# A two-layer attention and retention trunk on one core: norm weights moved from the tokens to the weights' rows, shorter rotary tables, a reordered first supertile

## The chip, the cores and the metric

The kernel runs on one core of a Trainium2 chip. Time is device microseconds of one execution. Before the change three runs took 2111.25 to 2114.31 us, median 2113.38. A change of 0.2% or less cannot be told from none.

The engines are called here as the profile calls them: PE (TensorE) multiplies matrices, DVE (VectorE) and ACT (ScalarE) work elementwise, POOL (GpSimd) too, and SP (SyncE) issues nearly all DMAs from its queue. Each engine works through its own instructions in order and waits for others by semaphores.

## The reference, cut to what matters

```python
D_MODEL = 1024; SEQ = 2048; DEPTH = 2; CHUNK = 64        # one batch
# per layer: 8 attention heads of 64, 4 retention heads of 128, w_in (1024, 4096), w_out (1024, 1024)

def rms_norm(x, gain=None):
    y = x * lax.rsqrt(jnp.mean(x * x, axis=-1, keepdims=True) + EPS)
    return y if gain is None else y * gain

def hybrid_layer(x, norm_gain, w_in, w_out, rel_bias, cos, sin):
    hn = rms_norm(x, norm_gain)
    aq, ak, av, ag, rq, rk, rv, rg = jnp.split(hn @ w_in, 8, axis=-1)
    ya = chunked_rel_attention(aq, ak, av, rel_bias)     # own chunk and 8 to the left, softmax
    yr = chunkwise_retention(rq, rk, rv, cos, sin)       # rotary on q and k, decaying state, RMS norm
    y = concatenate([ya * silu(ag), yr * silu(rg)], axis=-1)
    return x + y @ w_out

def reference(x, positions, norm_gain, w_in, w_out, rel_bias, final_gain):
    cos, sin = rotary_tables(positions, 128)             # angle = position * inverse frequency
    for layer in range(DEPTH):
        x = hybrid_layer(x, norm_gain[layer], w_in[layer], w_out[layer], rel_bias[layer], cos, sin)
    return rms_norm(x, final_gain)
```

The norm's weights multiply the columns of hn, which are the rows of w_in in the product: (n * gain) @ w is n @ (gain[:, None] * w).

## The kernel before

**Tiling.** There are 16 token tiles of 128 rows and four supertiles of 512 tokens (index n). The heads are cut into four groups s, each with two attention heads and one retention head. The main loop runs over layer l, group s and supertile n. Every large product is made in two float16 halves for accuracy: a matrix is split into an upper half (wh, hTh) and the rest (wl, hTl), and each product has three terms, upper by upper, upper by lower, lower by upper, over eight blocks of 128 rows (kt): 24 matmuls of 512 columns.

**Stages of one (l, s, n).** dense_T (line 608) makes q and k of attention and of retention with the weights as the stationary operand (matmuls of line 730; the first supertile of all goes by single token tiles, line 712, for its first two sections). evacuate copies each result out; for the retention sections it also turns q and k by the rotary tables: swap (line 664) loads the two halves exchanged by DMA, turn multiplies and adds on POOL (lines 670 to 672), upper, lower and third split the result, tokens transposes k. dense_V (line 737) makes the values and gates (matmuls of line 750). attention (line 776) and retention (line 863) of the supertile before run interleaved with these products: a unit of attention every three rounds, a round being eight dense matmuls.

Attention's unit: scores on PE (lines 798, 799), bias and maximum on DVE (802), exp and upper half on ACT (805, 807), lower half on POOL (808), a transposing DMA (810), and two units later the product with v on PE (818 to 820). A retention step multiplies k and q (line 853), masks the product on DVE (872), takes its upper half on ACT (857) and the rest on DVE (861), and multiplies these by v on PE (853 again).

**Order by hand.** PE, ACT, DVE and POOL run in program order. later(k, fn) puts an instruction k rounds ahead, and push(gen, steps) queues background work, of which run pulls a share in each round. SP's order is left to the scheduler, which issues a DMA as soon as its buffer is free, except up to the first supertile's dense_V, where it is program order as well.

**Background work.** prep_T and prep_V load the next group's eight weight sections of 128 columns (512 KB each; three buffers, w4), square them for a scale (309), sum the squares over partitions with a small matmul (323), and split them in two halves (330 on ACT, 333 on DVE). prep_T of the next group starts at n = 1, prep_V at n = 3; prep_V_next and a half-loading prep_T do it for the next layer during the output product. prep_Omax sums the squares of w_out from eight loads, pushed at s = 2, n = 0, and prep_O splits it. bias_scratch and bias_tiles make the group's bias tiles: a DMA spreads the bias in DRAM (564), another loads a skewed tile (577), POOL sets two corners (579, 580), ACT scales it (581); they are due in n = 0 of each group.

**Norms.** x is loaded by token tile, squared on ACT, and the root taken by POOL (212). Then DVE multiplies the tile by the root and by the gain row, which lies on all partitions as gains[l].b (line 254 for tokens 0 to 7, 1168 for 8 to 15, 986 for layer 1), and the product is split in halves and transposed: tokens 0 to 3 on PE, the others of layer 0 by two DMAs (236, 237); layer 1 by either. gain_scale (line 161) makes a power-of-two scale from the gain, which enters the root (g.m, g.e) and every section's inverse scale (g.i).

**Tables.** tables(n) computes sine and cosine of a supertile's angles in 17 steps on a 128 x 256 tile, mostly on DVE, in three to four floats' precision, stores them to DRAM by eight DMAs, and dense_T loads them back (616, 617).

**The start.** Up to the first dense_V everything is in one list of steps written out by hand (line 1348): x for tokens, W and V for sections, sq, hi, lo and so on for what is done, t for a step of the first tables, d for a step of dense_T, r for the bias's reversal. What follows (line 1353) is a list of 12 rounds beside the first dense_V, with tokens 4 to 7 and steps u of the second tables.

Of the kernel before, what the change touches and what calls it, by code (L numbers as in the profile page):

```python
# [27 lines left out]
def hybrid_trunk(ctx: ExitStack, tc: tile.TileContext, x, pos, gain, gcol, w_in, w_out, rel, fgain,  # L28
# [33 lines left out]
    pool.memset(mhalf, -0.5)  # L62
    invf_sb = cp.tile([P, 1], F32, tag="invf", name="invf_sb")
# [19 lines left out]
    def tables(n, wk):  # L83
# [15 lines left out]
        dve.tensor_copy(ang, pi)  # L99
        dve.tensor_scalar(ang, ang, invf_sb[:, 0:1], None, op0=ALU.mult)  # L100
# [6 lines left out]
        dve.tensor_scalar(k2, k, -(PD + PE_), None, op0=ALU.mult)  # L107
        dve.tensor_tensor(k2, k2, ang, op=ALU.add)
# [7 lines left out]
        dve.tensor_scalar(k, ang, HALF_PI, -TWO_PI, op0=ALU.is_gt, op1=ALU.mult)  # L116
# [19 lines left out]
    TAB_STEPS = 19  # L136
# [5 lines left out]
    def norm_scale(sq, nm, ig=None, k=14):  # L142
# [7 lines left out]
        if ig is not None:  # L150
            dve.tensor_tensor(i.bitcast(F32), i.bitcast(F32), ig, op=ALU.mult)
        return s.bitcast(F32), i.bitcast(F32)

    gains = {}

    def gain_load(l):
        g = gains[l]
        g.b = cp.tile([P, D], F32, tag="gb", name=f"gb{l}")
        sp.dma_start(g.b, gain[l:l + 1, :].to_broadcast([P, D]))

    def gain_scale(l):

        g = gains[l] = St()
        small = lambda tag, w=1, t=F32: b2.tile([P, w], t, tag=tag, name=f"{tag}{l}", bufs=1)
        m, gk = small("gsq", KT), small("gsk", KT)
        ss, i2, e2 = small("gss"), small("gs2", 1, I32), small("gs3", 1, I32)
        raw = gsb[:, l * KT:(l + 1) * KT]
        dve.tensor_tensor_reduce(out=m, in0=raw, in1=raw, scale=1.0, scalar=0.0, op0=ALU.mult, op1=ALU.add, accum_out=ss)
        mb = lowp(ss, f"g{l}")
        yield  # L170
        s_, i_ = norm_scale(allsum(mb, f"g{l}", 2.0 ** -60), f"g{l}", None, -1)
        g.i = b2.tile([P, 1], F32, tag="gi", name=f"gi{l}")
        dve.tensor_copy(g.i, i_)
        dve.tensor_scalar(gk, raw, s_[:, 0:1], None, op0=ALU.mult)
        dve.tensor_tensor(gk, gk, gk, op=ALU.mult)
        dve.tensor_tensor(gk, gk, gk, op=ALU.mult)
        dve.tensor_tensor_reduce(out=m, in0=gk, in1=gk, scale=1.0, scalar=0.0, op0=ALU.mult, op1=ALU.add, accum_out=ss)
        mb = lowp(ss, f"h{l}")
        yield
        m2 = allsum(mb, f"h{l}", 2.0 ** -60)  # L180
        dve.tensor_scalar(e2, m2.bitcast(I32), 23, None, op0=ALU.logical_shift_right)
        dve.tensor_scalar(e2, e2, 9.0, None, op0=ALU.add)
        dve.tensor_scalar(e2, e2, 3, 23, op0=ALU.logical_shift_right, op1=ALU.logical_shift_left)
        dve.tensor_scalar(i2, e2, float(111 << 23), None, op0=ALU.add)
        g.m = b2.tile([P, 1], F32, tag="gm", name=f"gm{l}")
        g.e = b2.tile([P, 1], F32, tag="ge", name=f"ge{l}")
        dve.tensor_tensor(g.i, g.i, i2.bitcast(F32), op=ALU.mult)
        dve.scalar_tensor_tensor(out=g.m, in0=g.i, scalar=2.0 ** -20 / D, in1=g.i, op0=ALU.mult, op1=ALU.mult)
        dve.scalar_tensor_tensor(out=g.e, in0=g.i, scalar=2.0 ** -20 * EPS, in1=g.i, op0=ALU.mult, op1=ALU.mult)
        yield  # L190
# [17 lines left out]
    def rms_of(ss, m, e, nm):  # L208

        dve.tensor_scalar(ss, ss, m, e, op0=ALU.mult, op1=ALU.add)  # L210
# [28 lines left out]
    class Tok:  # L239
# [10 lines left out]
        def rs(self):  # L250
            self.r = rms_of(self.ss, gains[0].m, gains[0].e, self.nm)

        def mul(self):
            dve.scalar_tensor_tensor(out=self.x, in0=self.x, scalar=self.r[:, 0:1], in1=gains[0].b, op0=ALU.mult,
                                     op1=ALU.mult)
# [10 lines left out]
        def hi(self):  # L266
            if self.rows:
                self.rw = (self.rows[:, 0:D], self.rows[:, D:2 * D])
                act.activation(self.rw[0], self.x, AF.Copy)
                return  # L270
# [3 lines left out]
        def lo(self):  # L274
            if self.rows:
                dve.tensor_tensor(self.rw[1], self.x, self.rw[0], op=ALU.subtract)
                return
# [73 lines left out]
    class Sections:  # L351
# [15 lines left out]

        def square(self, j):
# [3 lines left out]
        def scale(self, j):  # L372
            nm = f"{self.nm}{j}"
            self.sv[j], self.iv[j] = norm_scale(allsum(self.sq[j], nm), nm, gains[self.l].i)
# [7 lines left out]
    def prep_T(l, s, g, halves=False, w=None):  # L382
        w = w or Sections(l, s, g, halves)
        w.load(0)
        yield
        for j in range(4):
            if j < 3:
                w.load(j + 1)
            yield
            w.square(j)  # L390
            yield
            yield
            yield
            w.scale(j)
            yield from w.split(j)

# [17 lines left out]
    def prep_V(l, s, g):  # L414
# [16 lines left out]
        def rest(k):  # L431
            for _ in range(k):
                yield

        ld(0)
        ld(1)
# [825 lines left out]
    for t in range(1, 4):  # L1262
        x_in(t)
# [230 lines left out]
```

## Time and profile before

| | us |
|---|---|
| median of three runs | 2113.38 |
| the profiled execution | 2117.65 |
| its span, first to last instruction | 2115.9 |
| PE busy in the span | 2010.4 |
| DVE, ACT, POOL busy | 1253.8, 1139.1, 679.5 |

The profile is of one execution. A row of the timeline gives the start in us from the span's start, the duration in us, engine, line, operation and tiles, and in brackets how long the engine had been idle before it and what ended that. SPq is SP's queue. A row of the waits gives the total in us, the count and the longest. A row of groups ends with busy us, mean ns of one, and idle time before them. Matmuls overlap, so a matmul's spacing, not its duration, is its cost.

### The profile page before, as it was taken

To read this page: it belongs to the slowest core of one execution; us is meant where nothing else is said; L and a number is where in the kernel's file an instruction comes from. 1 tells how busy PE (TensorE), PEld (TensorE's weight loads), DVE (VectorE), ACT (ScalarE), POOL (GpSimd) and SP (SyncE) were. 2 spreads that over 40 slices of the span, in tenths; PEclk is the share of its full clock that TensorE was granted. 3 is DMA by queue.
4 is the path that set the end of the run, shared out by engine and by line. 5 is a ranking of instruction groups with operands and counts; after the bars stand their busy time and mean duration, and the time that the engine had idled before them with its cause. 6 is when DMAs were issued, how large, how long until landed. Compare 5 with 4: busy or idle time off the path is not lost.

```text
span 2115.9 us, 39456 instructions
## 1 busy us (share of the span) xinstructions
PE 2010.4 (95%) x14014; PEld 1052.1 (50%) x14014; DVE 1253.8 (59%) x3839; ACT 1139.1 (54%) x2522; POOL 679.5 (32%) x701
## 2 busy tenths in 40 slices
PE   6778999999999999988999999999999999999998
PEld 4334555555455555544444555555545555554543
DVE  7677566655565655566653556555656566556643
ACT  7455665556655654555444546554665465446432
POOL 1233333433343433321002343434333433433200
PEclk9899999999999999999999999999999999999999
DMA  8767675558665764699875556555685567548874
GB/s 247 165 119 164 137 164 113 115 110 191 148 113 111 159 158 99 132 197 259 206 187 115 121 103 140 123 124 103 149 186 119 101 137 169 123 101 182 217 193 127
DMA packets 645701, 313.63 MB, mean 148 GB/s; under 512 B 459232, under 2 KB 602080, under 8 KB 645504
## 3 DMA queue, kind: packets, MB, share of 16 engines
q1 hardware_dynamic: 645504, 311.12, 66.5%
q8 instruction: 109, 1.79, 0.4%
q14 instruction: 88, 0.72, 0.1%
HBM read 123.26 MB, written 41.98 MB: 78 GB/s over the span
## 4 chain that ended last, share of the span: by engine, by line
PE 47%; DMA 3%; ACT 2%; DVE 2%; issue 1%; POOL 1%; SPq 1%; POOLq 0%; DVEq 0%; ACTq 0%
PE dT L730 14%; PE dV L750 14%; PE dO L1090 12%; DMA pT<-pq 2%; PE r L853 2%; PE S L799 1%; PE S L798 1%; PE o L818 1%; PE o L819 1%; PE o L820 1%; DVE sc L802 1%; ACT sc L805 0%; ACT pq L807 0%; DMA yhy<-rhy 0%; DMA bias<-toep 0%
## 5 line engine op out<-in xcount | busy, mean ns | idle before, releaser
L808 POOL TENSOR_TENSOR pq<-sc,pq 128x640 f16<-128x640 f32 (+4 forms) x256 | 319.9, 1250 | 930.1 <-ACT pq L807 562.5
L805 ACT ACTIVATE sc<-sc,mq,cT 128x640 f32<-128x640 f32 (+4 forms) x256 | 218.5, 853 | 653.8 <-DVE rl L824 330.4
L730 PE MATMUL dT<-hTh,whT 128*128 128x512 f16 x1008 | 386.0, 383 | 11.9 <-DVE rv L766 7.8
L750 PE MATMUL dV<-wlV,hTh 128*128 128x512 f16 x1024 | 389.1, 380 | 6.9 <-DVE wlV L333 6.9
L750 PE MATMUL dV<-whV,hTh 128*128 128x512 f16 x1024 | 389.3, 380 | 6.2 <-DVE gt L768 6.1
L730 PE MATMUL dT<-hTl,whT 128*128 128x512 f16 x1008 | 386.2, 383 | 4.6 <-DMA hTl<-hTl 2.9
L750 PE MATMUL dV<-whV,hTl 128*128 128x512 f16 x1024 | 389.0, 380 | 0.0
L730 PE MATMUL dT<-hTh,wlT 128*128 128x512 f16 x1008 | 385.7, 383 | 0.0
L730 PEld LDWEIGHTS <-whT 128*128 128x128 f16 x2016 | 195.9, 99 | 236.7 <-issue 20.4
L750 PEld LDWEIGHTS <-hTh 128*128 128x128 f16 x2048 | 197.7, 98 | 223.9 <-DVE gt L768 9.1
L802 DVE CUSTOM_DVE_ANT_0 sc<-S,bias 128x640 f32<-128x640 f32 (+4 forms) x256 | 188.8, 737 | 154.7 <-PE S L799 150.8
L1090 PE MATMUL dO<-whO,yhy 128*128 128x512 f16 x512 | 194.8, 381 | 1.9 <-DMA yhy<-rhy 1.9
L1090 PE MATMUL dO<-whO,yly 128*128 128x512 f16 x512 | 194.6, 380 | 0.8 <-DMA yly<-rly 0.8
L1090 PE MATMUL dO<-wlO,yhy 128*128 128x512 f16 x512 | 194.6, 380 | 0.0
L807 ACT ACTIVATE pq<-sc 128x640 f16<-128x640 f32 (+4 forms) x256 | 171.5, 670 | 11.1 <-DMA pT<-pq 3.0
L1090 PEld LDWEIGHTS <-yhy 128*128 128x128 f16 x1024 | 99.9, 98 | 117.2 <-DMA yhy<-rhy 2.6
L750 PEld LDWEIGHTS <-hTl 128*128 128x128 f16 x1024 | 100.3, 98 | 115.8 <-issue 9.9
L730 PEld LDWEIGHTS <-wlT 128*128 128x128 f16 x1008 | 99.3, 98 | 106.4 <-issue 4.3
L818 PE MATMUL o<-v,pT 128*128 128x65 f16 x1120 | 129.8, 193 | 15.6 <-DMA pT<-pq 15.5
L798 PE MATMUL S<-k,q 128*128 128x128 f16 (+3 forms) x592 | 142.3, 267 | 0.7 <-DVE mq L802 0.7
L818 PEld LDWEIGHTS <-pT 128*128 128x128 f16 x1120 | 105.7, 97 | 51.0 <-DMA pT<-pq 21.5
L819 PE MATMUL o<-v,pT 128*128 128x64 f16 x1120 | 130.0, 195 | 0.0
(350 smaller groups left out, 3499.3 us busy)
## 6 DMA issues: line engine op xcount, KB each, us to landing
q<-qq SPq DMA_DIRECT2D x128, 128.0 KB, 2.5
yyy<-y_d SPq DMA_DIRECT2D x32, 512.0 KB, 4.6
stT<-in_w_in_dram SPq DMA_DIRECT2D x27, 512.0 KB, 4.8
stV<-in_w_in_dram SPq DMA_DIRECT2D x26, 512.0 KB, 4.4
k<-kk SPq DMA_DIRECT2D x128, 64.0 KB, 2.1
swp<-rot SPq DMA_DIRECT2D x64, 128.0 KB, 2.6
tabc<-tab SPq DMA_DIRECT2D x32, 256.0 KB, 2.7
tabs<-tab SPq DMA_DIRECT2D x32, 256.0 KB, 3.1
```

The source lines that it names most:

```text
L730: pe.matmul(ps, w_[:, j, kt, :], h_[:, kt, :], start=(m == 0), stop=(m == 23))
L750: pe.matmul(ps, h_[:, kt, a * P:(a + 1) * P], w_[:, kt, :], start=(m == 0), stop=(m == 23))
L798: pe.matmul(o, st.q[:, hx, 0, cs], k_, start=True, stop=False)
L799: pe.matmul(o, st.q[:, hx, 1, cs], k_, start=False, stop=True)
L802: dve.tensor_tensor_reduce(out=v, in0=S[:, 0:w], in1=g.bias[hx][:, 640 - w:640], scale=1.0, scalar=-3.0e38, op0=ALU.add, op1=ALU.max, accu ...
L805: act.activation(v, v, AF.Exp, bias=m[:, 0:1], scale=g.c[:, 0:1])
L807: act.activation(pq[:, 0:w], v, AF.Copy)
L808: pool.tensor_tensor(pq[:, w:2 * w], v, pq[:, 0:w], op=ALU.subtract)
L818: pe.matmul(o[:, 0:65], u.p[:, b, :], v_[:, 0:65], start=(b == 0), stop=False)
L819: pe.matmul(o[:, 0:64], u.p[:, b, :], v_[:, 65:129], start=False, stop=False)
L853: pe.matmul(out_, w_, m_, start=(i == 0), stop=(i + 1 == len(pairs)))
L1090: pe.matmul(ps, h_[:, kt, :], w_[:, kt, :], start=(m == 0), stop=(m == 23))
```

## The change

1. **Gain on the weights.** A new function multiplies a weight section by the norm's weights, one value per row, on DVE, before its squares are taken. It runs once for each of the 64 sections of w_in. The gain row on all partitions, its loads, gain_scale and the gain's scale in every inverse scale are gone. Tokens are no longer multiplied by the gain: where DMAs transpose them, the split takes the root as a scale and the multiplication is gone (12 tiles of layer 0, 10 of layer 1); where PE does, a one-input multiplication by the root stays (4 and 6).
2. **Tables.** Integer to float and the product with the frequency become one step on ACT; two pairs of DVE steps become one each; the cosine is taken as the sine of a quarter turn less the absolute angle; the negation goes to ACT.
3. **Order of terms.** For the first section of dense_T and the first tile of dense_V all eight blocks of one term come first, then the next term, with the half that is ready last at the end. Elsewhere dense_T takes the lower weights second and the lower tokens third.
4. **The first supertile.** The start's DMAs, its list of steps and the 12 rounds are ordered anew: the first weights before the positions, the table steps later, the swap of retention's k in round 9 and not 5 of dense_V, its upper, lower and transposition after it; the loads of tokens 8 to 11 explicitly in the rounds; retention's steps of this supertile in later rounds.
5. **Preparation.** prep_T loads two sections ahead, prep_V three; their lists are shorter by two steps and one.
6. **w_out's squares** are pushed at n = 2 of s = 2 and not n = 0.

```diff
+    def by_gain(st, k0, k1, l):
+
+        g = gsb[:, l * KT + k0:l * KT + k1].unsqueeze(2).to_broadcast([P, k1 - k0, P])
+        dve.tensor_tensor(st, st, g, op=ALU.mult)
...
-        dve.tensor_copy(ang, pi)
-        dve.tensor_scalar(ang, ang, invf_sb[:, 0:1], None, op0=ALU.mult)
+        act.activation(ang, pi, AF.Copy, scale=invf_sb[:, 0:1])
...
-        dve.tensor_scalar(k2, k, -(PD + PE_), None, op0=ALU.mult)
-        dve.tensor_tensor(k2, k2, ang, op=ALU.add)
+        dve.scalar_tensor_tensor(out=k2, in0=k, scalar=-(PD + PE_), in1=ang, op0=ALU.mult, op1=ALU.add)
...
-        dve.tensor_scalar(k, ang, HALF_PI, -TWO_PI, op0=ALU.is_gt, op1=ALU.mult)
-        yield
-        dve.tensor_tensor(k, k, ang, op=ALU.add)
-        dve.tensor_scalar(k, k, HALF_PI, PI_CL, op0=ALU.add, op1=ALU.min)
+        yield
+        dve.scalar_tensor_tensor(out=k, in0=ang, scalar=-1.0, in1=ang, op0=ALU.mult, op1=ALU.max)
...
-        act.activation(k2, k, AF.Sin)
+        act.activation(k2, k, AF.Sin, scale=-1.0, bias=quarter[:, 0:1])
...
-        dve.tensor_scalar(ang, r, -1.0, None, op0=ALU.mult)
+        act.activation(ang, r, AF.Copy, scale=-1.0)
...
     def prep_T(l, s, g, halves=False, w=None):
         w = w or Sections(l, s, g, halves)
-        w.load(0)
+        for j in range(2):
+            w.load(j)
+            yield
+        w.gain(0)
         yield
         for j in range(4):
+            w.square(j)
+            yield
+            yield
             if j < 3:
-                w.load(j + 1)
-            yield
-            w.square(j)
-            yield
-            yield
+                w.gain(j + 1)
             yield
             w.scale(j)
             yield from w.split(j)
+            if j < 2:
+                w.load(j + 2)
...
+    def in_order(apart, terms):
+
+        return [(kt, w) for w in terms for kt in range(KT)] if apart else [(kt, w) for kt in range(KT) for w in terms]
...
-                    d = 4 if j == 2 and first else 3
-                    later(d, turn)
-                    later(d + 2 if first else d + 3, upper)
-                    later(d + 3 if first else d + 4, lower)
...
+                    elif j == 2:
+                        plan = {4: turn, 11: upper, 12: lower, 13: third}
+                    else:
+                        plan = {3: turn, 5: upper, 6: lower, 7: tokens}
...
-                    later(5 if first else 2, swap)
+                    later(9 if first else 2, swap)
...
-                for (w_, h_) in ((g.h, hh), (g.h, hl), (g.l, hh)):
+            for kt, (w_, h_) in in_order(j == 0, ((g.h, hh), (g.l, hh), (g.h, hl))):
...
-                for (w_, h_) in ((g.vh, hh), (g.vl, hh), (g.vh, hl)):
+            for kt, (w_, h_) in in_order(a == 0, ((g.vh, hh), (g.vh, hl), (g.vl, hh))):
...
+        rounds_ret = (5, 10, 10, 14, 14, 18, 18, 23) if (l, s, n) == (0, 0, 0) else [6 * a + b for a in range(4) for b in (0, 5)]
...
         def mul():
-            u.x = xt if on_pe or rows else psS.tile([P, D], F32, tag="S", name=f"xn{nm}")
-            dve.scalar_tensor_tensor(out=u.x, in0=xt, scalar=u.rs[:, 0:1], in1=gains[l].b, op0=ALU.mult, op1=ALU.mult)
+            dve.tensor_scalar(xt, xt, u.rs[:, 0:1], None, op0=ALU.mult)
...
+    sp.dma_start(gsb, gcol)
     W = Sections(0, 0, g00, False)
-    sp.dma_start(gsb, gcol)
-    gains[0] = St()
-    gain_load(0)
+    W.load(0)
     sp.dma_start(invf_sb, invf)
+    x_in(1)
     t0 = tables(0, [gp.tile([P, 256], F32, tag="gt", name=f"wk{i}") for i in range(4)])
...
+    do("xsq0 xrs0 t xmul0 xtr0 Wgm0 xsq1 Wsq0 xrs1 xhi0 xmul1 Wlp0 Wsc0 xlo0 Whi0 xtr1 t xsq2 Wlo0 xrs2 d Wgm1 xhi1 xmul2 "
+       "Wsq1 xlo1 xtr2 Wlp1 xsq3 Wsc1 d xrs3 xhi2 Wgm2 Whi1 xlo2 Wsq2 xmul3 Wlo1 d t Wgm3 xtr3 r Wsq3 d xhi3 Vgm0 Wlp2 Wsc2 "
+       "xlo3 r d Vsq0 Whi2 Vgm1 Whi3 Wlo2 d Vsq1 Vlp0 Wlo3 Vsc0 bs t d Vhi0 t t d d Vhi1 Vgm2 t Vlo0 t Vsq2 d Vgm3 Vlo1 t Vsq3 "
+       "d Vlp2 t d Tu Vsc2 xsq4 t Vhi2 Vhi3 d t d Vlo2 t Vlo3 xsq5 t d Vu t d xsq6 xrs4 t d Vu t xsq7 d t")
     g00.vdone = 4
...
+    push(rounds(["xhi4 xrs5 xrs6", "xlo4 xrs7", "xdma4 xhi5 bt", "xlo5 xhi6", "xdma5 xlo6", "xdma6 xhi7",
+                 "xlo7", "xdma7 x8", "u x8 bt", "u u x8 bt", "u u x8", "u u bt"]), 12)
...
-                if n == 0 and s == 2:
+                if n == 2 and s == 2:
                     push(prep_Omax(l, go), 13)
```

More of the change, by code (lines that the diff above doesn't have):

```diff
@@ L62, in hybrid_trunk @@
     pool.memset(mhalf, -0.5)
+    quarter = cp.tile([P, 1], F32, tag="quarter", name="quarter")
+    pool.memset(quarter, HALF_PI)
     invf_sb = cp.tile([P, 1], F32, tag="invf", name="invf_sb")
@@ L366, in load, with gain @@
             self.sts.append(load_sec(w_in[self.l, :, o:o + P], f"{self.nm}{j}", self.halves))
+        def gain(self, j):
+            for (st, k0, k1) in self.sts[j]:
+                by_gain(st, k0, k1, self.l)
         def square(self, j):
@@ L455, in prep_V @@
         yield
-        yield from rest(2)
-        m = allsum(m2, f"{nm}2")
-        sv, iv[2] = norm_scale(m, f"{nm}2", gains[l].i)
+        yield
+        sv, iv[2] = norm_scale(allsum(m2, f"{nm}2"), f"{nm}2")
         for _ in V_units(l, s, g, iv, nm):
@@ L474, in prep_V_next @@
             sts.append([(st, 0, KT)])
+        for j in range(2):
+            for (st, k0, k1) in sts[j]:
+                by_gain(st, k0, k1, l)
         yield
+        for j in (2, 3):
+            by_gain(sts[j][0][0], 0, KT, l)
         g.vh = b3.tile([P, KT, 512], F16, tag="wh", name=f"wh{nm}")
@@ L727, in dense_T @@
             m = 0
[L728 to L733 removed]
+            for kt, (w_, h_) in in_order(j == 0, ((g.h, hh), (g.l, hh), (g.h, hl))):
+                pe.matmul(ps, w_[:, j, kt, :], h_[:, kt, :], start=(m == 0), stop=(m == 23))
+                m += 1
+                if m in (8, 16) or (m == 24 and first):
+                    yield
             evacuate(j, ps)
```

176 lines of the change are left out of this document (59 added, 117 removed), and 3 rows, old and new, of the table steps.

## The prediction

> **What bounds the kernel now.** I read the page first, then busy time by stretches.
>
> ```profile
> span 2115.9 us, 39456 instructions
> PE 2010.4 (95%) x14014; PEld 1052.1 (50%) x14014; DVE 1253.8 (59%) x3839; ACT 1139.1 (54%) x2522; POOL 679.5 (32%) x701
> ...
> 0.00:100.00 100.00, 72.92 (x491) 42.48 (x492) 69.32 (x181) 59.03 (x116) 18.88 (x35) 0.93 0.79 208
> 100.00:310.00 210.00, 181.34 (x1290) 94.14 (x1288) 140.54 (x417) 121.86 (x266) 78.27 (x76) 0.95 0.70 147
> 310.00:900.00 590.00, 579.28 (x4293) 309.14 (x4290) 347.83 (x1154) 332.42 (x776) 225.10 (x224) 1.00 0.62 132
> ```
>
> The columns of the last three are PE, PEld, DVE, ACT, POOL, granted clock, DMA share, GB/s. PE is the bound: it idles 2115.9 - 2010.4 = 105.5 us. Of that 27.1 us lie in the first 100 us and 28.7 in the next 210, all in the first supertile group (layer 0, s = 0); the following 590 us, three whole groups, idle 10.7. The multiply-adds are the same before and after (two orders of terms, no fewer), so the change can win only idle time and the slow clock behind it, and lose only by new idle time. The waits of PE, largest first, then name who ends them; the first three rows are of 100 to 310 us, the last of the whole run (total, times, longest):
>
> ```profile
> PE r L853 <- DVE dT L861: 11.7, 5, 5.3
> ...
> PE dT L730 <- DMA hTh<-rhn: 3.0, 1, 3.0
> ...
> PE dT L730 <- DMA hTl<-rln: 1.6, 2, 0.9
> ...
> PE dV L750 <- DVE wlV L333: 6.9, 5, 1.6
> ```
>
> **A, the start, to the first dense_V.** Removed: the load of the gain row to all partitions, ahead of the first weights, and gain_scale, whose last instruction sits at 8.51. Added: eight by_gain.
>
> ```profile
> 4.33 0.59 SPq L294 DMA_DIRECT2D stT<-in_w_in_dram  x1
> ...
> 5.30 0.19 ACT L248 ACTIVATION_READ_ACCUMULATOR hTh<-xa 128x1 f32 x1
> ...
> 8.51 0.15 DVE L189 SCALAR_TENSOR_TENSOR ge<-gi 128x1 f32<-128x1 f32 x1
> ...
> 11.40 1.06 ACT L1225 ACTIVATE whT<-stT 128x1024 f16<-128x1024 f32 x1 [5.92 <-DMA stT<-in_w_in_dram]
> ...
> 15.81 1.03 PE L712 MATMUL dT<-hTh,whT 128*128 128x128 f16 x8 [2.59 <-ACT whT L1307]
> ...
> 20.00:40.00 20.00, 18.19 (x226) 15.00 (x225) 18.99 (x46) 18.31 (x33) 0.69 (x1) 1.00 0.90 273
> ```
>
> The first weights set the first dense matmul, at 15.81. Their load moves from SP's place behind the gain row, invf and the positions to the place behind x0, the gain columns and the mask: some 2 us earlier. One by_gain now stands between landing and square. Its price has no row; the nearest is the two-input 1024-element form:
>
> ```profile
> L254 DVE SCALAR_TENSOR_TENSOR xa<-xa,rsn,gb 128x1024 f32<-128x1024 f32 x2 | 2.6, 1282 | 0.1
> ...
> L333 DVE SCALAR_TENSOR_TENSOR wlT<-stT,sT,whT 128x1024 f16<-128x1024 f32 (+1 forms) x32 | 38.0, 1197 | 6.9 <-ACT whT L330 6.8
> ...
> L93 DVE SCALAR_TENSOR_TENSOR wk<-wk,wk 128x256 f32<-128x256 f32 x8 | 3.4, 420 | 0.1
> ...
> 10.94 0.28 DVE L96 TENSOR_SCALAR wk<-wk 128x256 f32<-128x256 f32 x1
> ```
>
> I take 1.28. A one-input multiply by the row's scale (tokens 0 to 3, six of layer 1) has its row only at 256 elements, 0.28; between four times that (1.12) and the same fixed part as the two-input form (about 0.7, from 0.42 at 256 and 1.28 at 1024) I take 0.7. From 20 to 40 us DVE is busy 18.99 of 20, so DVE decides how soon the eight sections are split. Its sum: +8 x 1.28 = +10.2; four token multiplies shorter by 0.58 = -2.3; gain_scale's place on the path -3.2 (its end near 8.7, to the 5.5 at which x0's squares are done); some eight table steps of 0.42 moved behind the last section's scale, about -3.3; five small products with the gain's scale, at the 0.15 of the row at 8.51, -0.8. Net +0.6, as good as even, so the earlier load can come through in part. **A = -1**; ends -2.3 (only the earlier load counts) and +3 (each by_gain also waits for its section to land). The order "all of one term, then the next" gives the V split's lower halves 16 matmuls of slack, so those don't hold dense_V.
>
> **B, tokens 4 to 7 and the second supertile.**
>
> ```profile
> 57.05 1.36 SPq L236 DMA_TRANSPOSE hTh<-hTh  x1
> ...
> 57.41 1.22 DVE L276 TENSOR_TENSOR hTh<-hTh,hTh 128x1024 f16<-128x1024 f32 x1
> ...
> 64.55 0.48 SPq L666 DMA_DIRECT2D swp<-raw  x1
> ...
> 66.09 1.30 SPq L236 DMA_TRANSPOSE hTh<-hTh  x1
> ...
> 74.94 1.24 SPq L237 DMA_TRANSPOSE hTl<-hTl  x1
> ...
> 76.35 0.58 PE L730 MATMUL dT<-hTh,whT 128*128 128x512 f16 x1 [7.78 <-DVE rv L766]
> 79.87 0.59 PE L730 MATMUL dT<-hTl,whT 128*128 128x512 f16 x1 [2.94 <-DMA hTl<-hTl]
> ...
> 80.68 0.63 PE L730 MATMUL dT<-hTh,whT 128*128 128x512 f16 x1
> 81.10 0.63 PE L730 MATMUL dT<-hTl,whT 128*128 128x512 f16 x1
> ...
> 85.75 0.38 PE L730 MATMUL dT<-hTh,whT 128*128 128x512 f16 x1
> 85.97 0.38 PE L730 MATMUL dT<-hTl,whT 128*128 128x512 f16 x1
> ```
>
> The wait is put down to DVE, but DVE was long done; the transposes were not. Token 5's lower half is ready at 57.41 + 1.22 = 58.63, its transposes go out at 66.09: SP's queue stands behind the swap of line 666, which waits for the buffer of the first rotation. The change moves that swap from round 5 to round 9, behind all eight transposes, and drops the four multiplies ahead of them. Then four pairs of 2.8 us follow 57.05: the last would go out near 68 rather than 75. Against it, the tables' eight stores stand last in the hand-written list now, and the table load, which waits for them, is queued on SP ahead of token 4: I put this at +3. Upper halves arrive 4.3 earlier so; and as the lower halves of the tokens are first needed at the 17th matmul, the wait of 2.94 goes. That is -7.2; ACT does two more table steps in these rounds, so **B = -6**; ends -11 (both waits gone) and +1 (table load later than that, nothing won).
>
> **C, the rest of the group, to 310 us.**
>
> ```profile
> 117.84 2.24 DVE L1168 SCALAR_TENSOR_TENSOR hTl<-hTl,rsn,gb 128x1024 f32<-128x1024 f32 x1
> ...
> 118.96 2.24 POOL L671 TENSOR_TENSOR swp<-swp,tabs 128x512 f32<-128x512 f32 x1
> ...
> 121.39 1.30 DVE L116 TENSOR_SCALAR xb<-xb 128x256 f32<-128x256 f32 x1
> ```
>
> The longest wait for dT (5.3) ends right behind these on DVE's queue: a token multiply, stretched beside POOL's rotation, then two table steps. The change removes eight such multiplies here and some 1.8 us of DVE per table (cast, negation and two steps go to ACT or merge), and spreads the first supertile's retention over later rounds. ACT takes two more steps of about 0.4 per table, beside its own 58% load. Of 11.7 I take 7.5 away; of the waits for transposed tokens, 3.0 + 1.6, all but 0.6, since the upper half no longer waits for the multiply and the lower has 16 matmuls more. After a long wait matmuls start 0.43 apart, later 0.22 (80.68 to 81.10, 85.75 to 85.97): two such stretches less, some six matmuls each at 0.21 (an estimate; the one in B lasts longer), would be -2.6; I take -1.5. 7.5 + 4.0 + 1.5: **C = -13**; ends -19 (11.7 + 3.0 + 1.6 + 2.6) and 0.
>
> [...]
>
> **D, dense_V's first tile in later groups.** With the order changed for a = 0, the lower weights are needed after 16 matmuls, 16 x 0.22 = 3.5 us, and come 1.6 late at most: the five waits, 6.9 together, go if DVE is not over 1.9 later than now. **D = -6.5**; ends -6.9 and 0.
>
> **E, the sums of squares of w_out.** They move from s = 2, n = 0 to n = 2.
>
> ```profile
> 524.00 0.59 SPq L294 DMA_DIRECT2D stO0m<-in_w_out_dram  x1
> ...
> 527.15 1.63 SPq L577 DMA_DIRECT2D bias<-toep  x1
> ...
> 534.25 0.15 POOL L579 MEMSET bias<- 64x64 f32 x1 [3.82 <-DMA bias<-toep]
> ...
> 535.67 0.39 PE L853 MATMUL r<-rv,dT 128*128 128x128 f16 x2 [3.89 <-ACT dT L857]
> ...
> 1561.78 0.39 PE L853 MATMUL r<-rv,dT 128*128 128x128 f16 x2 [4.50 <-ACT dT L857]
> ...
> 730.00:750.00 20.00, 20.00 (x157) 10.85 (x155) 11.22 (x38) 12.98 (x32) 9.02 (x11) 1.00 0.73 161
> ```
>
> Eight 512 KB loads stand ahead of the bias tile; POOL waits for it, ACT's scaling of it waits for POOL, dT's upper half is queued behind that on ACT, PE waits 3.89, in layer 1 4.50. At the same place of s = 3, where no such loads are, PE is busy 20.00 of 20. With slow matmuls behind each (again some six or seven by 0.21) 11.2 stand there. At n = 2 no bias is loaded; the squares still crowd ACT. **E = -10**; ends -11.2 and 0.
>
> **F, layer 1's tokens.** Ten multiplies leave, six shorten.
>
> ```profile
> 999.17 1.30 PE L991 MATMUL ptn<-ident,hTh 128*128 128x128 f32 x8 [1.90 <-DVE hTh L986]
> ```
>
> Here a shortened one is waited for: -0.6, perhaps the slow start too. **F = -1**; ends -1.9 and 0. The end of the kernel is untouched.
>
> **G, the other 56 sections' by_gain**, 56 x 1.28 = 71.7 us of DVE, less 22 token multiplies (28). They lie in rounds with dense matmuls, where DVE is busy 59% (347.83 of 590), with two rounds between one and the next heavy step; the lower halves of line 333, 1.2 long and as many, lie there already and PE idles next to nothing. What is queued behind one: score evictions, dense evictions, dT's rest, each with a round or two of slack (a round of 8 matmuls is 1.7). **G = +4**; ends 0 and +71.7. The shorter prep lists, the earlier section loads and the three loads of prep_V cost nothing: buffers, not program order, release them. Should that cover fail, a by_gain waits on its load and G is where it shows.
>
> **Sum.** -1 - 6 - 13 - 6.5 - 10 - 1 + 4 = -33.5. The profiled execution took 2117.65, 1.75 outside its span: 2084 there. The median of the runs, 2113.38, is 4.3 lower: **2080 us**.
>
> **Rivals.** *All waits go*: A to F at their far ends, -2.3 - 11 - 19 - 6.9 - 11.2 - 1.9 = -52.3, G nothing: 2061. For: DVE's share outside the first group; against: each wait has a next one behind it. *The first group gains nothing* because DVE, saturated there, or the later table stores give back what they win: A, B, C at 0, 2113.4 - 13.5 = 2100. For: 18.99 of 20. *The change doesn't do what it says*: the next group's section loads stand ahead of the bias in place of w_out's; E = 0, 2090. Against: s = 3 of today. *Slower*: by_gain, in the same queue as dT's rest, and stretched where it meets POOL (2.24 against 1.28 above), makes dT late in each prep round. Without G the sum is -37.5; it decides from 37.5 / 56 = 0.67 us of PE per by_gain; at its full 1.28 the time is 2113.4 - 37.5 + 71.7 = 2148. For: the two rows of 2.24; against: line 333's neighbours today.
> [...]
>
> **Chances.** Forecast 0.50; first group gains nothing 0.17; all waits go 0.13; w_out's move wins nothing 0.08; slower 0.07; about the same 0.05. This kernel's measurement tells 0.2% (4.2 us) from nothing. Faster 0.87, same 0.05, slower 0.08. The range, 2058 to 2106, takes in the first four cases with the spread of their terms and leaves out the last two.
>
> **What would show it.** B: SP's eight transposes without the swap among them, no wait on hTl. C: the waits of line 853 for dT under 4. D: no row of wlV. E: none at 530 and 1560 for ACT's dT. G: new rows of PE on dT or gt between 310 and 900. Wrong, if the idle time of 310 to 900 us grows past 20, or dense_V starts well after 48 us.

## The result, and the profile after

The changed kernel is slower: 2145.07 us (median of four runs, 2143.94 to 2148.42) against 2113.85 (four runs, 2111.25 to 2117.63), a ratio of 1.015 with an interval of 1.013 to 1.017. The prediction was 2080, its range 2058 to 2106. The profiled execution took 2148.42 us, its span is 2146.4, 30.5 more than before; both profiled executions are the slowest of their four.

The page of the changed kernel, span and busy time:

```profile
span 2146.4 us, 39352 instructions
...
PE 2030.4 (95%) x14010; PEld 1057.5 (49%) x14010; DVE 1270.6 (59%) x3765; ACT 1145.4 (53%) x2530; POOL 688.0 (32%) x702
```

DVE is busy only 17 us more than before (1270.6 - 1253.8): the removed multiplications and table steps nearly pay for by_gain. PE idles 116.0 us (2146.4 - 2030.4) and not 105.5; the other 20 us are busy time of the same matmuls, at a lower mean clock (0.980 granted, 0.987 before). The waits of PE in the changed kernel (total, times, longest) name what is new:

```profile
PE o L798 <- DMA pT<-pq: 26.0, 13, 3.8
PE msT L285 <- DVE ya L810: 16.9, 6, 3.3
PE r L832 <- DVE sh L840: 8.1, 4, 6.0
...
PE r L832 <- ACT dT L836: 3.3, 2, 2.1
```

Attention's product with v (o) waited 15.5 us for its transposing DMA before, now 26.0. The second row is new: the small matmul of a weight section's scale (msT, line 285) waits for attention's last DVE step, six times (before, the one of prep_V did so twice, 1.8 us in all). The last row is the squares of w_out at their new place. No row of wlV is left (6.9 before). By stretches the loss lies where the prediction saw none:

```profile
0.00:100.00 100.00, 75.14 (x488) 43.70 (x489) 60.42 (x137) 59.80 (x117) 18.63 (x35) 0.93 0.75 201
100.00:310.00 210.00, 186.44 (x1340) 97.89 (x1339) 137.04 (x413) 129.21 (x282) 82.38 (x80) 0.95 0.70 148
310.00:900.00 590.00, 573.52 (x4187) 303.79 (x4186) 349.53 (x1110) 320.92 (x748) 223.67 (x219) 0.99 0.59 127
```

PE is busy 7 us more in the first 310 us and 6 us less in the next 590, where idle time goes from 10.7 to 16.5. Below, stage times are the starts of the first matmul of every dense_T and dense_V in the two timelines; a step is what a stage gained or lost between two such starts. All steps of the two profiled executions, grouped by the parts of the prediction:

| part | predicted, us | measured, us | from |
|---|---|---|---|
| A, start to first dense_V | -1 | +5.6 | 53.33 against 47.69 |
| B, to dense_V of the second supertile | -6 | -6.2 | -7.9 at its dense_T, +1.8 behind |
| C, to 310 us | -13 | -3.0 | six steps |
| D and E, terms and squares | -16.5 | -15.9 | -6.2 (s = 1, 3), -15.2 (s = 2, dense_V of n = 0 and the dense_T behind it), +5.5 (squares' new place) |
| F, layer 1's tokens | -1 | -0.7 | output stages |
| G, by_gain elsewhere | +4 | +50.6 | +32.9 at the end of five n = 1, +17.7 in five n = 0 |
| sum | -33.5 | +30.5 | before rounding; spans: +30.5 |

F can't be told from nothing: the step with layer 1's tokens is -0.3 us here, and -4.3 in no_gain_t and +5.1 in late_scale below, which treat these tokens alike.

**How one of the five stalls comes about.** The timeline of the changed kernel, all engines, at the end of n = 1 of s = 1:

```profile
354.55 2.30 DVE L153 TENSOR_TENSOR stT<-stT,gsb 128x1024 f32<-128x1024 f32 x1
...
355.85 2.13 POOL L654 TENSOR_TENSOR raw<-raw,swp 128x512 f32<-128x512 f32 x1
...
357.33 0.38 PE L779 MATMUL S<-k,q 128*128 128x512 f16 x1
...
358.60 0.15 DVE L146 TENSOR_SCALAR sT<-eT 128x1 int32<-128x1 int32 x1
...
358.78 1.15 ACT L292 ACTIVATE whT<-stT,sT 128x1024 f16<-128x1024 f32 x1 [2.14 <-DVE sT L146]
...
360.75 0.29 DVE L744 SCALAR_TENSOR_TENSOR v<-dV,v 128x128 f16<-128x128 f32 x1 [1.94 <-ACT rv L740]
...
362.94 0.68 DVE L782 CUSTOM_DVE_ANT_0 sc<-S,bias 128x512 f32<-128x512 f32 x1
...
363.91 0.81 ACT L785 ACTIVATE sc<-sc,mq,cT 128x512 f32<-128x512 f32 x1 [2.34 <-DVE mq L784]
364.22 0.38 PE L779 MATMUL S<-k,q 128*128 128x512 f16 x1
...
365.29 1.04 ACT L271 ACTIVATE whT<-stT 128x1024 f16<-128x1024 f32 x1
...
366.45 0.16 DVE L278 CAST mbT<-m1T 128x1 bf16<-128x1 f32 x1 [2.58 <-ACT whT L271]
...
367.52 0.28 DVE L810 SCALAR_TENSOR_TENSOR ya<-o,rl,gt 128x64 f32<-128x64 f32 x1
...
367.86 0.18 PE L285 MATMUL msT<-mbT,ones 128*128 128x1 bf16 x1 [3.26 <-DVE ya L810]
...
368.97 0.63 PE L730 MATMUL dV<-whV,hTl 128*128 128x512 f16 x1
369.40 0.63 PE L730 MATMUL dV<-wlV,hTh 128*128 128x512 f16 x1
```

DVE and ACT hand work to each other and each waits about 2 us at every hand-over (the brackets). by_gain, stretched from 1.2 to 2.3 beside POOL, makes the scale (358.60) late, and so does the small step of line 805 behind it, 1.03 instead of 0.16 beside POOL's 2.13; ACT's upper half waits for it, dense_V's copies are behind that on ACT, the eviction of the scores behind those on DVE: scores made at 357.33 are evicted at 362.94, 5.6 us later. So ACT squares the next section late, the cast of its sum stands on DVE ahead of attention's last step, and PE, which had done the scores by 364.6, has the small matmul next in its queue: by the code it takes one of the four PSUM buffers that attention's output and the retention use too, and that step of attention frees one. It waits 3.26, and eight matmuls behind it start 0.43 apart, as the last two rows do, and not 0.22: another 1.7. With a wait of 0.66 for the scale, at 358.37, PE waits 3.9 of this step's 5.9 us; in all five steps it waits 19.6 of the 32.9, and nearly all the rest is slow matmuls. That rest varies: late_scale, early_pos and no_gain_v below keep prep_T as it is, wait 18.0 to 20.2 there and lose 24.4 to 26.7. The kernel before, same group:

```profile
368.63 0.38 PE L799 MATMUL S<-k,q 128*128 128x512 f16 x1
...
369.78 0.16 DVE L316 CAST mbT<-m1T 128x1 bf16<-128x1 f32 x1 [1.67 <-ACT whT L309]
...
370.58 0.17 PE L323 MATMUL msT<-mbT,ones 128*128 128x1 bf16 x1
...
371.81 0.68 DVE L802 CUSTOM_DVE_ANT_0 sc<-S,bias 128x512 f32<-128x512 f32 x1
```

There the small matmul comes a round behind the scores, the cast is done at 369.94, 0.6 us before it, and the eviction follows its scores by 3.2 us. The margin that the prediction called a round or two was 0.6 us at this place, and this fence, from the trace of before, would have shown it.

### The profile page after: what moved, and what is told of

It is laid out like the page before. It is cut to its first block, busy times and chain, and to the rows that moved or that the text cites. A ratio compares the mean times of both kernels' runs of the same rounds, so it can differ in the third digit from the quotient of the medians.

```text
span 2146.4 us, 39352 instructions
## 1 busy us (share of the span) xinstructions
PE 2030.4 (95%) x14010; PEld 1057.5 (49%) x14010; DVE 1270.6 (59%) x3765; ACT 1145.4 (53%) x2530; POOL 688.0 (32%) x702
## 5 line engine op out<-in xcount | busy, mean ns | idle before, releaser
L711 PE MATMUL dT<-hTh,whT 128*128 128x512 f16 x1008 | 352.3, 385 | 11.8 <-issue 6.3
L730 PE MATMUL dV<-whV,hTh 128*128 128x512 f16 x1024 | 357.1, 384 | 3.3 <-DVE gt L748 2.3
L730 PE MATMUL dV<-wlV,hTh 128*128 128x512 f16 x1024 | 357.4, 385 | 0.0
L730 PE MATMUL dV<-whV,hTl 128*128 128x512 f16 x1024 | 356.7, 384 | 0.0
L711 PE MATMUL dT<-hTl,whT 128*128 128x512 f16 x1008 | 350.9, 383 | 0.0
L711 PE MATMUL dT<-hTh,wlT 128*128 128x512 f16 x1008 | 350.8, 383 | 0.0
L711 PEld LDWEIGHTS <-whT 128*128 128x128 f16 x2016 | 194.4, 99 | 230.7 <-issue 17.7
L730 PEld LDWEIGHTS <-hTh 128*128 128x128 f16 x2048 | 197.7, 99 | 223.9 <-issue 12.5
L778 PE MATMUL S<-k,q 128*128 128x128 f16 (+3 forms) x592 | 143.7, 269 | 0.8 <-DVE mq L782 0.7
L779 PE MATMUL S<-k,q 128*128 128x128 f16 (+3 forms) x592 | 131.2, 269 | 0.0
```

Source lines behind the costliest of these rows:

```text
L711: pe.matmul(ps, w_[:, j, kt, :], h_[:, kt, :], start=(m == 0), stop=(m == 23))
L730: pe.matmul(ps, h_[:, kt, a * P:(a + 1) * P], w_[:, kt, :], start=(m == 0), stop=(m == 23))
L778: pe.matmul(o, st.q[:, hx, 0, cs], k_, start=True, stop=False)
L779: pe.matmul(o, st.q[:, hx, 1, cs], k_, start=False, stop=True)
```

## The experiments

**Multiplication or list?** prep_T changed in two ways: by_gain came in, and a section got five rounds and not six. Three kernels take these apart. The first leaves the multiplications out of prep_T (no_gain_t):

```diff
-        w.gain(0)
         yield
...
-            if j < 3:
-                w.gain(j + 1)
             yield
```

> Leaves out the multiplication by the norm's weights in prep_T of later groups (its four steps of the list stay, empty), so those sections lack the gain. Theory TIME (each by_gain, 1.2 to 2.4 us, stands on DVE ahead of the scale and the scores while DVE and ACT already run some three rounds behind PE, so the small matmul of the next scale finds no free PSUM buffer): the five stalls at the end of n = 1, 5.9 + 7.1 + 5.7 + 7.0 + 7.2 = 32.9 us, go, 2145 - 33 = 2112 us. Theory SPACING (the new list gives a section five rounds instead of six, and that makes DVE late): they stay, 2143 to 2146, the wait of 3.3 on the attention output among them.

Measured: 2118.2 us, against before 1.0011 (0.9999 to 1.0024). The five steps at the end of n = 1 fall from 32.9 to 6.9 us; the waits of PE have

```profile
PE msT L285 <- DVE ya L807: 6.1, 5, 1.9
```

So by_gain is needed for most of the stall, though 6.9 us stay without it. The second keeps by_gain and gives a section six rounds again (wide_t):

```diff
-        push(prep_T(l, s + 1, grp(l, s + 1)), 23)
+        push(prep_T(l, s + 1, grp(l, s + 1), wide=n == 1), 27 if n == 1 else 23)
...
             if j < 2:
                 w.load(j + 2)
+            if wide:
+                yield
```

> The changed kernel, prep_T at n = 1 with one empty step after each section (six rounds a section as before, running three rounds into n = 2), gains kept. Theory SPACING: the stalls at the end of n = 1 go, 2112 us. Theory TIME: by_gain of the last section still stands ahead of the scale; most of the stall stays, 2130 to 2145 us.

Measured: 2114.66 us, 1.0005 (0.9995 to 1.0015). The steps at the end of n = 1 are 0.0 each, with every multiplication in place. In its waits and its timeline:

```profile
PE msT L285 <- DVE ya L812: 0.6, 1, 0.6
```
```profile
370.70 0.16 DVE L278 CAST mbT<-m1T 128x1 bf16<-128x1 f32 x1 [2.64 <-ACT whT L271]
...
372.14 0.17 PE L285 MATMUL msT<-mbT,ones 128*128 128x1 bf16 x1
```

Here the small matmul stands right behind the scores as in the changed kernel, but the cast is 1.3 us ahead of it. The four cases together, the five steps of n = 1 summed (the kernel before is the zero):

| | no multiplication in prep_T | with it |
|---|---|---|
| six rounds a section | 0 (the kernel before) | 0.0 |
| five rounds a section | 6.9 | 32.9 |

Neither theory alone: the shorter list uses up the margin, by_gain goes beyond it. Six rounds change one thing more, though. With five, the last multiplication of each stalled group lies beside POOL and takes 2.29 to 2.30 us; with six, none of prep_T takes over 1.23. Whether the room or the missed meeting with POOL wins is not parted: no run has five rounds and no such meeting. The third moves the next multiplication behind the lower half of the section before (gain_after):

```diff
-            if j < 3:
-                w.gain(j + 1)
             yield
             w.scale(j)
-            yield from w.split(j)
+            for k, _ in enumerate(w.split(j)):
+                if k == 1 and j < 3:
+                    w.gain(j + 1)
+                yield
```

> The changed kernel, prep_T's next multiplication issued behind the lower half of the section before it and not ahead of its scale, five rounds a section as in the changed kernel. Theory PLACE (it hurts by standing ahead of the scale, on which ACT's upper half waits 2.1 us): the five stalls fall from 32.9 to the 6.9 us that were left without the multiplications, 2145 - 26 = 2119 us. Theory TIME (any place in those five rounds makes DVE late): they stay within a third, 2134 to 2145 us.

Measured: 2138.37 us, 1.0114 (1.0092 to 1.0137); the five steps sum to 23.9, of which 15.0 are waits. In five rounds the place matters little; TIME holds against PLACE. At the new place too one multiplication a group meets POOL (1.93 to 2.29 us).

**The waits of n = 0.** The multiplications are left out of prep_V (no_gain_v):

```diff
         def gn(j):
-            for (st, k0, k1) in sts[j]:
-                by_gain(st, k0, k1, l)
+            pass
```

> Leaves out the multiplication by the norm's weights in prep_V, so those sections lack the gain. Theory TIME (by_gain delays the scores' eviction, so exp, its split and the transposing DMA of attention's weights come late): the waits of the attention product on that DMA in dense_T of n = 0 (3.1 us at 714 and alike) go with their slow matmuls, stages 1.6 + 1.7 + 5.7 + 3.1 + 1.9 + 2.8 = 17 us: 2128 us. Theory DMA (three section loads issued at once crowd the transposing DMA): they stay, 2145 us.

Measured: 2127.8 us, 1.0063 (1.0048 to 1.0078), as TIME has it; the five groups' steps of n = 0 fall from 17.7 to 3.8. The changed kernel's timeline at n = 0 of s = 3, where dense_T starts at 696.31, then the same place without the multiplications, where it starts at 690.32:

```profile
695.91 0.81 DVE L782 CUSTOM_DVE_ANT_0 sc<-S,bias 128x640 f32<-128x640 f32 x1
...
700.32 1.33 SPq L790 DMA_TRANSPOSE pT<-pq  x1
...
707.17 0.34 SPq L555 DMA_DIRECT2D bias<-toep  x1
...
708.43 3.62 SPq L790 DMA_TRANSPOSE pT<-pq  x1
...
714.66 0.24 PE L798 MATMUL o<-v,pT 128*128 128x65 f16 x1 [3.11 <-DMA pT<-pq]
```
```profile
687.39 0.82 DVE L781 CUSTOM_DVE_ANT_0 sc<-S,bias 128x640 f32<-128x640 f32 x1
...
691.80 1.34 SPq L789 DMA_TRANSPOSE pT<-pq  x1
...
700.68 2.85 SPq L789 DMA_TRANSPOSE pT<-pq  x1
...
705.79 0.20 PE L797 MATMUL o<-v,pT 128*128 128x65 f16 x1 [0.53 <-DMA pT<-pq]
```

Two multiplications of prep_V (at 678.58, 2.23 us long, and at 687.35) make DVE late: from the start of dense_T, the eviction comes 2.5 us later than without them, and so does its transpose. On SP's queue the bias's DMAs stand behind that transpose, and behind these the next one, which goes out 1.8 us later, though POOL had its data ready 2.8 us before. From there to the product it is 6.2 us and not 5.1. The three loads at once are not needed for this: they are still there in the second fence. The next kernel, on the one with six rounds, moves the first three multiplications of prep_V ahead into dense_T of n = 3 (early_v):

```diff
+    def ahead_V(l, s, g):
+        g.vst = [load_sec(w_in[l, :, VSEC[j] * 512 + s * P:VSEC[j] * 512 + s * P + P], f"V{l}_{s}{j}") for j in range(3)]
+        yield
+        for j in range(3):
+            yield
+            yield
+            for (st, k0, k1) in g.vst[j]:
+                by_gain(st, k0, k1, l)
+            yield
...
+                if n == NS - 1 and s + 1 < NSW and (l, s) != (0, 0):
+                    push(ahead_V(l, s + 1, grp(l, s + 1)), 11)
```

> The kernel with six rounds a section in prep_T (2114.7 us), and the first three of prep_V's sections loaded and multiplied in dense_T of n = 3, ahead of the squares (not in the first group). Theory TIME: the waits for the transposing DMA at n = 0 go but in the first group, 1.7 + 3.6 + 3.3 + 1.5 + 2.4 = 12.5 us: 2102 us. Theory DMA (three loads at once crowd the transposes): they stay, since the loads only move away from n = 3's second half: 2112 to 2115 us.

Measured: 2105.82 us, 0.9964 (0.9947 to 0.9981), 8.8 us less than with six rounds alone, of 12.5 expected. Its five runs lie between 2099.39 and 2109.30, the profiled one lowest. In that one the five groups' steps of n = 0 sum to -1.2, and to 15.0 in the one with six rounds alone: what the change lost there is gone, though waits of 1.1 to 2.2 us for the transposes stay, as before the change (0.5 to 2.3). Here too no multiplication meets POOL any more; two of prep_V did in each group (2.23 and 2.43 us), so that part is not separated either.

**Parts of the change on the kernel before.** D and E alone (before_de):

```diff
-            for kt in range(KT):
-                for (w_, h_) in ((g.vh, hh), (g.vl, hh), (g.vh, hl)):
+            for kt, (w_, h_) in in_order(a == 0, ((g.vh, hh), (g.vh, hl), (g.vl, hh))):
...
-                if n == 0 and s == 2:
+                if n == 2 and s == 2:
                     push(prep_Omax(l, go), 13)
```

> The kernel before with two parts of the change alone: the order of terms of dense_V's first tile, and w_out's squares at n = 2 of s = 2. By the prediction 6.5 + 10 us less: 2097 us. By the changed kernel's stages -7.5 for the terms, -12 + 5.4 for the squares: 2100 us. Rival, that both are given back at the next wait: 2114 us.

Measured: 2101.98 us, 0.9941 (0.9924 to 0.9958): 12.3 us less. The steps agree with the changed kernel's to 0.9 us: -6.2 and -1.4 at s = 2 of layer 0, +2.3 at the squares' new place, -1.5 where wlV was waited for in s = 3.

**The start.** The third V scale's small matmul, moved three dense_T steps back (late_scale):

```diff
-        "d Vlp2 t d Tu Vsc2 xsq4 t Vhi2 Vhi3 d t d Vlo2 t Vlo3 xsq5 t d Vu t d xsq6 xrs4 t d Vu t xsq7 d t")
+        "d Vlp2 t d Tu d xsq4 t d t d Vsc2 t Vhi2 Vhi3 Vlo2 Vlo3 xsq5 t d Vu t d xsq6 xrs4 t d Vu t xsq7 d t")
```

> The changed kernel, in the start's list the third V scale (its small matmul waits on PE for DVE's cast at 44.6 us, 4.3 us) three dense_T steps later. Theory ORDER (dense_V starts 5.6 us later than before only since that matmul stands too early in PE's queue): wait and its slow matmuls go, dense_V's first matmul near 49 and not 53.3 us, 2145 - 4.5 = 2140.5 us. Theory LOAD (DVE's 10 us of by_gain are what makes the start longer): PE waits later for the V split instead, dense_V still near 53 us, 2145 us.

Measured: 2145.77 us, 1.0156 (1.0141 to 1.0171): nothing won, though ORDER holds. Its timeline, dense_V's start and then the second supertile's:

```profile
49.01 1.24 PE L730 MATMUL dV<-whV,hTh 128*128 128x512 f16 x5 [0.86 <-ACT whV L1278]
...
73.39 1.87 PE L711 MATMUL dT<-hTh,whT 128*128 128x512 f16 x4 [2.90 <-DMA hTh<-hTl]
```

dense_V starts 4.3 us earlier and PE gives it back at the next wait, for the tokens' transposes: the second supertile starts at 73.39, against 74.05 in the changed kernel, where dense_V ran until then. So A's loss cost 0.7 us at most: A and B are one term, bounded by those transposes. The next one moves the load of the second tables' positions ahead of the last token's transposes (early_pos):

```diff
-                 "xlo7", "xdma7 x8", "u x8 bt", "u u x8 bt", "u u x8", "u u bt"]), 12)
+                 "xlo7 u", "xdma7 x8", "x8 bt", "u u x8 bt", "u u x8", "u u bt"]), 12)
```

> The changed kernel, the load of the second tables' positions two rounds earlier, ahead of the last token's transposes. Theory QUEUE (ACT stands 8.5 us behind its new cast step, which waits for that load; dense_V's copies behind it, then DVE, then PE 5.6 us at 85): the wait at 85 us goes, with its slow matmuls 7 us, 2138 us; 2 us of it may return at the transposes. Rival (DVE's own 16 us of the tables and rotation there set it): under 2 us, 2143 to 2145 us.

Measured: 2145.57 us, 1.0151 (1.0132 to 1.0169). The changed kernel's timeline, then this one's:

```profile
79.54 0.51 ACT L101 ACTIVATE xa<-xa,invf_sb 128x256 f32<-128x256 int32 x1 [8.51 <-DMA xa<-in_pos_dram]
...
85.07 0.61 PE L711 MATMUL dT<-hTh,whT 128*128 128x512 f16 x1 [5.56 <-DVE gt L748]
```
```profile
73.38 0.51 ACT L101 ACTIVATE xa<-xa,invf_sb 128x256 f32<-128x256 int32 x1 [2.55 <-DMA xa<-in_pos_dram]
...
84.67 0.83 ACT L559 ACTIVATE bias<-bias,ciT 128x640 f32<-128x640 f32 x1 [9.14 <-POOL bias L558]
...
87.32 0.29 PE L832 MATMUL r<-rot,rot 128*128 128x128 f16 x2 [1.88 <-ACT rot L657]
```

QUEUE is right about the wait: the cast that the change put on ACT stood 8.51 us behind its load, and the 5.56 behind it go. But ACT then stands behind the bias tile, 9.14, and PE behind ACT: 1.0 us is left at the second supertile's dense_V, none in the median.

**All of it.** Six rounds, V's multiplications ahead, both moves of the start, and w_out's squares two rounds apart (21 steps, pushed before dense_T of n = 2) (all_moved):

```diff
         for j in range(KT):
+            yield
             yield
             m1 = sumsq(st, f"{nm}m{j}", None)
```

> All of it: six rounds a section, V's multiplications early, the third V scale later, the positions earlier, and w_out's squares over 21 rounds of n = 2 and not 13. If the causes are separate the gains add: 2114.7 - 12.5 - 4.5 - 7 - 4.5 (the squares' own cost at n = 2) = 2086 us. If each is given back at the next wait, 2100 us or more.

Measured: 2096.60 us, 0.9926 (0.9911 to 0.994), between the two expectations. The n = 1 and n = 0 parts add; the squares' cost falls from 5.5 to 2.0 us; the start gives its part back, as above. On top of it, tokens 8 to 15 get row buffers of their own (own_rows):

```diff
-            us[k].rows = row_pair(us[k].nm)
+            us[k].rows = [b1.tile([P, D], F16, tag=f"own{i}", name=f"own{i}{us[k].nm}") for i in range(2)]
```

> The kernel with all parts moved (2096.6 us), the two row buffers of tokens 8 to 15 apart from attention's score buffers. Theory SHARED BUFFER (the score eviction at 111 us waits 1.8 us on DVE for the transposing DMA of a token, and the retention's rest queued behind it makes PE wait 6 us at 110 to 116; that is why C did not come with the multiplications gone): that wait falls under 2 us, 4 to 6 us from the stretch 100 to 210 us, 2091 to 2093 us. Rival (DVE's load there, beside POOL's rotation): the wait stays, 2095 to 2097 us.

Measured: 2092.15 us, 0.990 (0.9882 to 0.9918), the best of all. The changed kernel's timeline at the longest of C's waits, then this one's:

```profile
111.31 0.56 DVE L782 CUSTOM_DVE_ANT_0 sc<-S,bias 128x384 f32<-128x384 f32 x1 [1.81 <-DMA hTh<-rhn]
...
116.53 0.26 PE L832 MATMUL r<-sh,rot 128*128 128x128 f16 x1 [6.00 <-DVE sh L840]
```
```profile
112.12 0.29 PE L848 MATMUL r<-rv,dT 128*128 128x128 f16 x2 [2.54 <-ACT dT L852]
...
115.45 0.26 PE L848 MATMUL r<-sh,rot 128*128 128x128 f16 x1 [2.93 <-DVE sh L856]
```

The wait parts into two, 5.5 us together: little is won here, and the expectation of under 2 us is missed. The 4.5 us of the median come at the fourth supertile (steps lower by 2.1 at its dense_T and 4.2 behind it): the wait for its tokens falls from 4.6 to 2.0, and 14 matmuls that started 0.43 apart behind that wait and the next are at 0.22 again. Finally the kernel before with the orders of terms, the spread squares and the first supertile's swap and retention in later rounds, but norms, tables and the start's list as they were (before_more):

```diff
-                    later(5 if first else 2, swap)
+                    later(9 if first else 2, swap)
...
-            for kt in range(KT):
-                for (w_, h_) in ((g.h, hh), (g.h, hl), (g.l, hh)):
+            for kt, (w_, h_) in in_order(j == 0, ((g.h, hh), (g.l, hh), (g.h, hl))):
...
+        rounds_ret = (5, 10, 10, 14, 14, 18, 18, 23) if (l, s, n) == (0, 0, 0) else [6 * a + b for a in range(4) for b in (0, 5)]
```

> The kernel before with the order of terms in dense_V and dense_T, the squares over 21 rounds of n = 2, and the first supertile's swap, split and retention in their later rounds; norms on the tokens, tables and the start's list as before. Theory SWAP (the swap in round 5 holds SP's queue and so the transposes of tokens 5 to 7): dense_T of n = 1 starts 4 to 8 us earlier, 2102 - 6 - 3 = 2093 us. Rival (the multiplications of these tokens and the later table stores set it): under 2 us there, 2098 to 2100 us.

Measured: 2092.91 us, 0.9903 (0.9884 to 0.9921). The step to dense_T of n = 1 is -2.8 us, that to its dense_V -1.2 (4 to 8 expected, under 2 by the rival: between them). So the parts that need no by_gain bring the kernel before to the same time as the best with it.

## Why the prediction was wrong

**G is the step that failed**, in two sentences of it. "Score evictions, dense evictions, dT's rest, each with a round or two of slack": busy time of 59% said nothing of how late DVE ran; scores were evicted 3.2 us behind PE already and the cast stood 0.6 us ahead of its matmul. "The shorter prep lists ... cost nothing: buffers, not program order, release them": true of the loads and wrong of the rest, for the list sets how close a section's DVE and ACT steps follow each other. With six rounds a section, and none of them beside POOL, 20 multiplications of prep_T cost nothing; with five, and one a group beside POOL, the step costs 32.9 us, 6.9 of it without any multiplication. by_gain itself was sized well where it runs alone, 1.22 against 1.28, but not beside POOL; the changed kernel's groups show it:

```profile
L153 DVE TENSOR_TENSOR stV<-stV,gsb 128x1024 f32<-128x1024 f32 (+1 forms) x30 | 45.2, 1518 | 0.0
L153 DVE TENSOR_TENSOR stT<-stT,gsb 128x1024 f32<-128x1024 f32 (+1 forms) x35 | 43.4, 1248 | 4.0 <-DMA stT<-in_w_in_dram 4.0
```

The V sections' mean is 1.52, with half tiles among them; 15 of the 70 take 2.23 to 2.44, and all of these lie beside POOL's rotation or split; eight others overlap its split and take 1.21 to 1.22. POOL's step beside the 2.30 is longer too, 2.13 against 1.27 in the median.

**The slower rival** had the right sign, the queue and POOL's part, and its 2148 is near. Its mechanism is only half of it: dT was hardly late; what was late were the small matmul and attention's transposes. And there is no price per multiplication: 50.6 / 56 = 0.9 us is above its point of 0.67, but with other lists (early_v) the same multiplications cost next to nothing.

**A** missed by 6.6 us, since the third V scale's matmul stood in PE's queue ahead of its cast (4.3 us; the other 2.3 are not accounted for); that it cost nothing in the end, the prediction could not say, because it took A and B for two terms. **B** is right in number by luck: PE came 5.6 us late into it, which by itself takes that much off the wait for the transposes. A and B together won 0.5 us of the 7 forecast. Its mechanism is partly right: the swap is not among the transposes any more and there is no wait on hTl, but the last transpose went out at 71.45 and not near 68, and a new wait came from the cast on ACT, which the prediction had put at "two more table steps". In before_more, where dense_V starts 1.1 us later than in the kernel before, the same two steps won 3.9.

**C** failed in size, 3.0 of 13: the multiplications are gone, but the waits only changed their names. dT's row of 5.3 became sh's of 6.0 at the same place, with shared row buffers, ACT's order and POOL's rotation still there; the wait for the fourth supertile's tokens grew from 3.0 to 4.8, and by_gain of the first group's own preparation lies in this stretch too. The 6.2 us that own_rows won over all_moved at the fourth supertile show the shared buffer as one cause; the others are seen in the timeline and were not tried.

**D and E** were right in mechanism: no wlV row, no wait for dT behind the bias tile; before_de alone won 12.3 us in the median. That the size fits, 15.9 of 16.5 us, is partly luck: the old place gave 15.2, D's share there included, where E counted 10, and E's remark that the squares "still crowd ACT", which the sum had at nothing, took 5.5 us at n = 2 (2.0 when spread). **F** is not resolved. The prediction's chances don't quite add up: its four faster cases make 0.88, not 0.87. Of the signs that the prediction named, the new rows of PE came, on msT and o and not on dT or gt; dense_V did start well after 48 us, at no cost in the end; the idle time of 310 to 900 us stayed under 20 (16.5), although the stages lost 15.6 us there: a bound on idle time misses the matmuls that start 0.43 and not 0.22 us apart behind the waits.

## What to carry to other kernels

Slack is read from the trace as the time between a producer's end and its consumer's start at the tightest place of the round, not from an engine's busy share. A background list's spacing is part of its cost: before adding work to a step or shortening the list, look which in-order engine stands behind the step that comes closest, and whether the added step meets POOL there: here 15 that did took 2.2 to 2.4 us and not 1.2. A wait that is removed is worth only the distance to the next one (dense_V 4.3 us earlier in late_scale won 0.7 at most); where two neighbouring stages end on the same transfer they are one term.

## What the runs showed of the hardware

The same wait of 2.81 us, for the same cast, had slow matmuls behind it in one kernel and none in another. all_moved, then own_rows, timeline of PE:

```profile
222.38 0.16 PE L285 MATMUL msT<-mbT,ones 128*128 128x1 bf16 x1 [2.81 <-DVE mbT L278]
...
223.20 0.63 PE L727 MATMUL dT<-hTh,whT 128*128 128x512 f16 x1
223.63 0.63 PE L727 MATMUL dT<-hTh,wlT 128*128 128x512 f16 x1
```
```profile
217.54 0.16 PE L285 MATMUL msT<-mbT,ones 128*128 128x1 bf16 x1 [2.81 <-DVE mbT L278]
...
218.00 0.38 PE L727 MATMUL dT<-hTl,whT 128*128 128x512 f16 x1
218.21 0.38 PE L727 MATMUL dT<-hTh,whT 128*128 128x512 f16 x1
```

Starts 0.43 apart in the first and 0.22 in the second. So a wait's length alone does not tell what it costs; what else decides it, no run shows. The prediction's six slow matmuls behind each long wait, an estimate, are no constant: five start 0.43 apart behind the wait of all_moved, none behind that of own_rows, eight behind the 3.26 of the changed kernel at 367.86, and seven behind the 1.90 of the kernel before at 999.17.
